# Weights' sums in three steps, queued by hand behind VectorE's products of later query units

## The chip, the cores and the metric

One core of one Trainium2 chip. The metric is the device time of one execution in microseconds; lower is better. Engines: TensorE (PE, with its weight load PEld), VectorE (DVE), ScalarE (ACT), GpSimd (POOL) and SyncE (SP), which issues the transfers.

## The reference

Two layers over a sequence of 1024 rows of width 1024 in float32: first windowed attention with a gate, then a gated linear recurrence (HGRN2) with 8 heads of 128 x 128 state. The second layer is where the change lies:

```
def hgrn2_mixer(h, lower_bound, w_in, gnorm_w, w_out):
    proj = h @ w_in
    q, f, i, z = jnp.split(proj, [FORGET_DIM, 2 * FORGET_DIM, 2 * FORGET_DIM + REC_WIDTH], axis=-1)
    q = jax.nn.silu(q)
    log_f = jnp.logaddexp(jnp.log(lb), jnp.log1p(-lb) + jax.nn.log_sigmoid(f))
    k = -jnp.expm1(log_f)
    ...
    o = chunked_gated_recurrence(q, k, v, log_f)
    o = o * lax.rsqrt(jnp.mean(o * o, axis=-1, keepdims=True) + NORM_EPS) * gnorm_w
    o = o.reshape(B, T, REC_WIDTH) * jax.nn.silu(z)
    return o @ w_out
```

## The kernel before

Matrix products are made of three float32 products of 128 x 128 by 128 x 512 each, from high and low parts (`acth`, `actl` for activations, `whi`, `wlo` for weights). A weight tile of 128 x 512 is loaded by SyncE into one of four `wraw` tiles (`fetch`), and split by ScalarE (`whi`, L203) and VectorE (`wlo`, L204) into one of ten slots as soon as TensorE has used the slot's former content up.

`mixer1` makes the second layer's recurrence. A *query unit* (`qf_unit`) is one product of 24 matmuls: per head four of them, the query and the gate, each for two halves of the sequence, in the order query, gate, query, gate. ScalarE takes a sigmoid of the PSUM bank, and for the query VectorE multiplies both (L946); that frees the bank, of which there are two for this, for the unit after the next. `rec(h)` is the recurrence of a head: two scans U and V on VectorE (L1013, L1014), products into the query and key (L1015, L1016, L1032 to L1036, L1062, tt), small products of TensorE (psd L1044, pss L1054, psq L1070, transposes pst L1087, psk L1093), the state S (L1097, L1099) and the outputs pso (L1106, L1108), which VectorE multiplies by rstd from GpSimd (L1114). `i_unit` makes the values.

The last two products, by the gate's weights z and the output's weights o, are done in the manner of Strassen and Winograd with seven products in place of eight, so sums of the weights' four quarters are needed. `weight_sums(k, ...)` makes them for a quarter tile k, four for z and four for o: it loads three quarters into the three tiles `p1z` (called b11, b12, b22), makes three sums on VectorE (L1127 or L1129, L1130, L1131), stores them to DRAM (`tz`, `td`), loads the remaining quarter into b12, makes a fourth sum (L1137) and stores it (L1138). The same three tiles serve all eight, and later hold first parts of the product z.

The order of the work is set by the list `plan` and a scheduler, which sorts what it is given by a model of its own; each engine's queue is then run in order. `tc.issue_after(ins)` makes the scheduler put instructions behind `ins` on the queue of its engine. `behind` uses it for the place on SyncE's queue: a tile's transfers stand behind the last weight load issued so far.

Of the kernel before, what the change touches and what calls it, by code (L numbers as in the profile page):

```python
# [18 lines left out]
ALU = mybir.AluOpType  # L19
# [71 lines left out]
def emit(tc, I, out):  # L91
    nc = tc.nc
    v = InOrder(tc, nc.vector)
# [7 lines left out]
    with top:  # L101
# [11 lines left out]
        tz, td, sd = [[dp.tile([4 * P, 512], F32, name=f"{n}{i}") for i in range(4)] for n in ("tz", "td", "sd")]  # L113
# [24 lines left out]
        QZ, QO = (100, 108, 104, 112), (120, 128, 116, 124)  # L138
# [15 lines left out]
        W = {"phase": 0, "pos": 0, "bank": 0, "plan": [], "split": 0, "fetch": 0, "left": {}, "place": {}, "dmas": {}, "split_ins": {}, "free": list(zip(whi, wlo))}  # L154
# [103 lines left out]
        def proj_feat(first, half, tag="mm", then={}):  # L258

            ps = mm(tag=tag)  # L260
            for k in range(NK):
                c = (k % 4) * P
                product(ps, k, weight(first, k // 4, c, c + P), act[k, half])
                used(first + k // 4)
                then.get(k, lambda: None)()
            return ps
# [655 lines left out]
        def mixer1(fast, vo, rp, p1z):  # L922
            def i_unit(c, t):
                ps = proj_nat(52 if c == 0 else 76, t)
                nc.scalar.activation(vo[c][:, t, :], ps, AF.Copy)
# [8 lines left out]
            def qf_unit(h, isf, half):  # L934
                ps = proj_feat(60 + 4 * h + 2 * isf + 8 * (h // 4), half)
                cs = slice(half * 512, (half + 1) * 512)
                if (h, isf) not in qfk:
                    if isf and fast:
                        qfk[h, 1] = Fs[h % 2]
                    else:  # L940
                        qfk[h, isf] = rp.tile([P, T], F32, tag="qf"[isf], bufs=2 if isf else nb3, name="qf")
                dst = qfk[h, isf][:, cs]
                if not isf:
                    sg = rp.tile([P, 512], F32, tag="sg", bufs=2, name="sg")
                    nc.scalar.activation(sg, ps, AF.Sigmoid)
                    v.tensor_tensor(dst, ps, sg, op=ALU.mult)  # L946
                else:
                    if (h, 2) not in qfk:
                        qfk[h, 2] = rp.tile([P, T], F32, tag="k", bufs=nb3, name="kk")
                    kk = qfk[h, 2][:, cs]  # L950
                    lb, ol = lbt[:, 1, h:h + 1], lbt[:, 0, h:h + 1]
                    nc.scalar.activation(dst, ps, AF.Sigmoid)  # L952
                    nc.scalar.activation(kk, ps, AF.Sigmoid, scale=-1.0)
                    nc.gpsimd.tensor_scalar(dst, dst, ol, lb, op0=ALU.mult, op1=ALU.add)  # L954
                    nc.gpsimd.tensor_scalar(kk, kk, ol, 1.0, op0=ALU.mult, op1=ALU.mult)
# [159 lines left out]

            QF = [(0, 0), (1, 0), (0, 1), (1, 1)]
            qf = lambda h: [lambda u=u: qf_unit(h, *u) for u in QF]
            iu = lambda c: [lambda t=t: i_unit(c, t) for t in range(8)]

            def weight_sums(k, quarters, dst, neg):  # L1120

                b11, b12, b22 = p1z
                for q, x in zip(quarters, (b11, b12, None, b22)):
                    if x is not None:
                        nc.sync.dma_start(x, I["w"][q + k])
                if neg:
                    v.tensor_tensor(b22, b12, b22, op=ALU.subtract)  # L1127
                else:
                    v.tensor_tensor(b22, b22, b12, op=ALU.subtract)  # L1129
                v.tensor_tensor(b12, b12, b11, op=ALU.subtract)  # L1130
                v.tensor_tensor(b11, b11, b22, op=ALU.subtract if neg else ALU.add)  # L1131
                r = slice(k * P, (k + 1) * P)
                for d, x in ((3, b12), (0, b22), (1, b11)):
                    nc.sync.dma_start(dst[d][r], x)
                b21 = b12
                nc.sync.dma_start(b21, I["w"][quarters[2] + k])
                v.tensor_tensor(b21, b21, b11, op=ALU.subtract)  # L1137
                nc.sync.dma_start(dst[2][r], b21)  # L1138

            rc = lambda h: [lambda: rec(h)]  # L1140

            wz, wo = ([lambda k=k, q=q, d=d, n=n: behind(weight_sums, k, q, d, n) for k in range(4)] for q, d, n in ((QZ, tz, True), (QO, td, False)))

            def behind(f, *a):

                with tc.issue_after(W["dmas"][W["fetch"] - 1].ins):
                    f(*a)

            def ahead(h):
                with tc.high_priority(offset=1200):  # L1150
                    rec(h)
# [4 lines left out]
                    first_part(t, p1z[t])  # L1156

            i1 = iu(1)
            plan = iu(0) + qf(0) + ([zeros] if fast else []) + qf(1) + wz[:1] + rc(0) + qf(2) + wz[1:2] + rc(1) + qf(3) + wz[2:3]
            plan += rc(2) + i1[:4] + wz[3:] + i1[4:] + wo[:1] + rc(3) + qf(4) + wo[1:2] + qf(5) + wo[2:3] + rc(4) + qf(6)  # L1160
            plan += wo[3:] + rc(5) + qf(7) + [lambda: ahead(6), first_parts, lambda: ahead(7)]
            for u in plan:
                u()
            if fast:
# [198 lines left out]
        def network(fast):  # L1363
            keep, oc = layer0()
            with pool("vo", "left") as vp:
                vo = [o0.rearrange("p a (b c) -> p (a b) c", b=2), vp.tile([P, 8, 512], F32, name="vo1")]
                with pool("fin0", "right") as fp:
                    output0(oc, fp, vo[1])
                keep.close()
                with pool("p1z", "right") as zp:  # L1370
                    p1z = [zp.tile([P, 512], F32, name=f"p1z{t}") for t in range(3)]
                    with pool("rec", "left") as rp:
                        final1(vo, rp, p1z, mixer1(fast, vo, rp, p1z))
# [109 lines left out]
```

## Time and profile before

| | |
|---|---|
| three runs | 891.12, 892.0, 892.0 us, median 892.0 |
| the profiled execution's own time | 890.71 us |
| its span, from first to last instruction | 889.0 us |
| TensorE busy | 861.7 us (97%) |
| VectorE busy | 645.7 us (73%) |
| ScalarE, GpSimd busy | 453.9, 313.5 us |
| mean granted clock of TensorE | 0.996 |

The weights' sums run from 466.5 us (the first load) to 669.2 us (the last store). An engine's waits are idle time in front of an instruction, put down to what ended it; a matmul's end is modelled, so TensorE's starts tell more than its ends.

### The profile page before, as it was taken

The numbers are of one execution on the slowest core, as the hardware profiler recorded it, in microseconds if no ns is written. First come the engines' busy times: TensorE is split into PE (matmuls) and PEld (weight loads), VectorE is DVE, ScalarE is ACT, GpSimd is POOL, SyncE is SP. The second block draws the span as 40 slices with busy tenths as digits, with TensorE's granted clock in tenths as the row PEclk, the third lists the DMA queues.
The fourth block names the chain that finished last, engine by engine and source line by source line (L and its number), as shares of the span: only waits on it lengthen the run. The fifth ranks groups of instructions, "written<-read, shape, count | busy, mean of one in ns | idle before, by whom it ended". The sixth has DMA issues, their size and how long they took to land.

```text
span 889.0 us, 14613 instructions
## 1 busy us (share of the span) xinstructions
PE 861.7 (97%) x5166; PEld 715.4 (80%) x5166; DVE 645.7 (73%) x1059; ACT 453.9 (51%) x1143; POOL 313.5 (35%) x475
## 2 busy tenths in 40 slices
PE   6999999999999999999999999999998999999995
PEld 5878888888888878788888788888886878887884
DVE  7898887677898436765279777248768966869985
ACT  5645777767788332753322341243242654668441
POOL 4543644655666303310054442114254421000032
PEclk9999999999999999999999999999999999999999
DMA  9766455313232134536213233063340445423244
GB/s 335 278 187 203 130 172 149 92 52 94 57 93 83 48 94 144 180 119 235 86 48 131 84 120 130 25 190 102 124 166 13 142 144 167 140 74 95 94 142 171
DMA packets 72924, 114.12 MB, mean 128 GB/s; under 512 B 7048, under 2 KB 27144, under 8 KB 72840
## 3 DMA queue, kind: packets, MB, share of 16 engines
q1 hardware_dynamic: 72560, 113.01, 39.2%
q8 instruction: 43, 0.70, 0.3%
q14 instruction: 41, 0.34, 0.1%
q10 hardware_dynamic: 280, 0.07, 0.0%
HBM read 81.76 MB, written 29.46 MB: 125 GB/s over the span
## 4 chain that ended last, share of the span: by engine, by line
PE 69%; DVE 16%; DMA 4%; issue 4%; ACT 3%; POOL 2%; SPq 0%; DVEq 0%; POOLq 0%; ACTq 0%
PE psmm L246 39%; PE psmm L88 17%; PE pss L88 3%; PE pso L88 2%; DMA p1z<-in_w 2%; PE pso L1106 2%; PE pst L88 1%; PE pso L1108 1%; DVE U L1013 1%; PE psk L1093 1%; POOL rstd L285 1%; DVE sc L1048 1%; DVE V L1014 1%; DVE kk L1016 1%; DVE qf L1015 1%
## 5 line engine op out<-in xcount | busy, mean ns | idle before, releaser
L246 PE MATMUL psmm<-whi,acth 128*128 128x512 f32 x448 | 176.9, 396 | 2.6 <-ACT o L1221 1.3
L246 PE MATMUL psmm<-wlo,acth 128*128 128x512 f32 x448 | 175.1, 391 | 0.0
L246 PE MATMUL psmm<-whi,actl 128*128 128x512 f32 x448 | 173.8, 392 | 0.0
L204 DVE TENSOR_TENSOR wlo<-wraw,whi 128x512 fp32r<-128x512 f32 x144 | 99.0, 700 | 64.4 <-ACT whi L203 63.7
L203 ACT ACTIVATE whi<-wraw 128x512 fp32r<-128x512 f32 x136 | 83.7, 628 | 82.5 <-PE psmm L246 63.3
L88 PE MATMUL psmm<-acth,whi 128*128 128x512 f32 x272 | 110.7, 407 | 1.7 <-ACT whi L88 1.7
L88 PE MATMUL psmm<-actl,whi 128*128 128x512 f32 x272 | 107.6, 396 | 0.2 <-DVE actl L88 0.2
L88 PE MATMUL psmm<-acth,wlo 128*128 128x512 f32 x272 | 107.7, 396 | 0.0
L246 PE MATMUL psmm<-acth,whi 128*128 128x512 f32 x256 | 101.9, 398 | 2.8 <-DVE qf L946 2.8
L246 PEld LDWEIGHTS psmm<-whi,acth 128*128 128x128 f32 x448 | 84.2, 188 | 20.6 <-DVE y L851 1.9
L246 PE MATMUL psmm<-acth,wlo 128*128 128x512 f32 x256 | 100.5, 393 | 0.0
L246 PE MATMUL psmm<-actl,whi 128*128 128x512 f32 x256 | 100.4, 392 | 0.0
L246 PEld LDWEIGHTS psmm<-whi,actl 128*128 128x128 f32 x448 | 84.1, 188 | 17.3
L246 PEld LDWEIGHTS psmm<-wlo,acth 128*128 128x128 f32 x448 | 84.2, 188 | 16.5
L736 ACT ACTIVATE sm<-sm,st 128x129 f32<-128x129 f32 x128 | 49.9, 392 | 25.9 <-DVE st L734 25.9
L88 PEld LDWEIGHTS psmm<-acth,wlo 128*128 128x128 f32 x272 | 51.7, 190 | 11.7 <-DVE wlo L88 0.2
L88 PEld LDWEIGHTS psmm<-acth,whi 128*128 128x128 f32 x272 | 52.0, 191 | 10.4 <-ACT whi L88 2.0
L246 PEld LDWEIGHTS psmm<-acth,whi 128*128 128x128 f32 x256 | 48.3, 189 | 14.4 <-DVE qf L946 4.4
L88 PEld LDWEIGHTS psmm<-actl,whi 128*128 128x128 f32 x272 | 51.9, 191 | 8.7 <-DVE actl L88 0.7
L246 PEld LDWEIGHTS psmm<-acth,wlo 128*128 128x128 f32 x256 | 48.3, 189 | 10.1
L246 PEld LDWEIGHTS psmm<-actl,whi 128*128 128x128 f32 x256 | 48.4, 189 | 9.5
L954 POOL TENSOR_SCALAR gate<-gate,lbt 128x512 f32<-128x512 f32 x16 | 20.0, 1251 | 90.2 <-ACT gate L952 90.2
(334 smaller groups left out, 1755.8 us busy)
## 6 DMA issues: line engine op xcount, KB each, us to landing
wraw<-in_w SPq DMA_DIRECT2D x124, 256.0 KB
QS<-qd SPq DMA_DIRECT2D x16, 512.0 KB
p1z<-in_w SPq DMA_DIRECT2D x32, 256.0 KB
xr<-in_x SPq DMA_DIRECT2D x8, 512.0 KB
x1d<-xn SPq DMA_DIRECT2D x8, 512.0 KB
tz<-p1z SPq DMA_DIRECT2D x16, 256.0 KB
td<-p1z SPq DMA_DIRECT2D x16, 256.0 KB
wraw<-sd SPq DMA_DIRECT2D x16, 256.0 KB
```

Source lines behind the costliest of these rows:

```text
L88: return (lambda *a, **k: self.tc.keep_in_program_order(f(*a, **k))) if self.on else f
L203: nc.scalar.activation(hi, raw, AF.Copy)
L204: W["split_ins"][i] = v.tensor_tensor(lo, raw, hi.bitcast(F32), op=ALU.subtract)
L246: W["mm"] = pe.matmul(ps, a, b, start=(k == first and i == 0), stop=(k == last and i == 2), skip_group_check=first is None)
L285: W["rstd"] = keep(g.tensor_tensor(r, m, nhalf[:, :width], op=ALU.pow))
L736: W["exp"] = nc.scalar.activation(sm[:, h, :], sm[:, h, :], AF.Exp, bias=nm[:, h:h + 1], scale=-1.0, accum_out=dn[:, h:h + 1])
L954: nc.gpsimd.tensor_scalar(dst, dst, ol, lb, op0=ALU.mult, op1=ALU.add)
L1013: v.tensor_tensor_scan(U, F[:, :T], F1, 0.0, op0=ALU.mult, op1=ALU.add)
L1014: v.tensor_tensor_scan(V[:, ::-1], F[:, T:0:-1], E1[:, ::-1], 0.0, op0=ALU.mult, op1=ALU.add)
L1015: v.tensor_tensor(Q, Q, U, op=ALU.mult)
L1016: v.tensor_tensor(K, K, V, op=ALU.mult)
L1106: nc.tensor.matmul(po[:, i, :], sc[:, c, :], vt[:, c, hc], start=True, stop=(c == 0))
```

## The change

`weight_sums` returns three steps that stand in the plan by themselves: `loads` (three transfers, behind the last weight load on SyncE's queue), `three` (three sums and their stores, and the load of the fourth quarter) and `fourth` (the last sum and its store). `W["q"]` is the last L946; the sums of `three` and `fourth` are put behind it on VectorE's queue. A function `qfs` sets the steps between a head's query units: the fourth step of the tile before and the loads of this tile behind the first unit, the three sums behind the third. Each tile of z goes with heads 1, 2, 3 and the values' units; each tile of o with heads 4 to 7, in place of behind heads 3 to 6; the last fourth sum stands behind all units of head 7. Lines of the new file: the sums L1127, L1129, L1130, L1131 and L1137 are L1134, L1136, L1137, L1138 and L1145 there. What is computed does not change.

```diff
--- before.py
+++ after.py
@@ -943,7 +943,7 @@
                 if not isf:
                     sg = rp.tile([P, 512], F32, tag="sg", bufs=2, name="sg")
                     nc.scalar.activation(sg, ps, AF.Sigmoid)
-                    v.tensor_tensor(dst, ps, sg, op=ALU.mult)
+                    W["q"] = v.tensor_tensor(dst, ps, sg, op=ALU.mult)
                 else:
                     if (h, 2) not in qfk:
                         qfk[h, 2] = rp.tile([P, T], F32, tag="k", bufs=nb3, name="kk")
@@ -1117,34 +1117,44 @@
             qf = lambda h: [lambda u=u: qf_unit(h, *u) for u in QF]
             iu = lambda c: [lambda t=t: i_unit(c, t) for t in range(8)]
 
+            b11, b12, b22 = p1z
+
             def weight_sums(k, quarters, dst, neg):
 
-                b11, b12, b22 = p1z
-                for q, x in zip(quarters, (b11, b12, None, b22)):
-                    if x is not None:
-                        nc.sync.dma_start(x, I["w"][q + k])
-                if neg:
-                    v.tensor_tensor(b22, b12, b22, op=ALU.subtract)
-                else:
-                    v.tensor_tensor(b22, b22, b12, op=ALU.subtract)
-                v.tensor_tensor(b12, b12, b11, op=ALU.subtract)
-                v.tensor_tensor(b11, b11, b22, op=ALU.subtract if neg else ALU.add)
                 r = slice(k * P, (k + 1) * P)
-                for d, x in ((3, b12), (0, b22), (1, b11)):
-                    nc.sync.dma_start(dst[d][r], x)
-                b21 = b12
-                nc.sync.dma_start(b21, I["w"][quarters[2] + k])
-                v.tensor_tensor(b21, b21, b11, op=ALU.subtract)
-                nc.sync.dma_start(dst[2][r], b21)
+
+                def loads():
+                    with tc.issue_after(W["dmas"][W["fetch"] - 1].ins):
+                        for q, x in ((0, b11), (1, b12), (3, b22)):
+                            nc.sync.dma_start(x, I["w"][quarters[q] + k])
+
+                def three():
+                    with tc.issue_after(W["q"].ins):
+                        if neg:
+                            v.tensor_tensor(b22, b12, b22, op=ALU.subtract)
+                        else:
+                            v.tensor_tensor(b22, b22, b12, op=ALU.subtract)
+                        v.tensor_tensor(b12, b12, b11, op=ALU.subtract)
+                        v.tensor_tensor(b11, b11, b22, op=ALU.subtract if neg else ALU.add)
+                    for d, x in ((3, b12), (0, b22), (1, b11)):
+                        nc.sync.dma_start(dst[d][r], x)
+                    nc.sync.dma_start(b12, I["w"][quarters[2] + k])
+
+                def fourth():
+                    with tc.issue_after(W["q"].ins):
+                        v.tensor_tensor(b12, b12, b11, op=ALU.subtract)
+                    nc.sync.dma_start(dst[2][r], b12)
+
+                return loads, three, fourth
 
             rc = lambda h: [lambda: rec(h)]
 
-            wz, wo = ([lambda k=k, q=q, d=d, n=n: behind(weight_sums, k, q, d, n) for k in range(4)] for q, d, n in ((QZ, tz, True), (QO, td, False)))
-
-            def behind(f, *a):
-
-                with tc.issue_after(W["dmas"][W["fetch"] - 1].ins):
-                    f(*a)
+            wz, wo = ([weight_sums(k, q, d, n) for k in range(4)] for q, d, n in ((QZ, tz, True), (QO, td, False)))
+
+            def qfs(h, now, last=None):
+
+                u = qf(h)
+                return u[:1] + ([last[2]] if last else []) + [now[0]] + u[1:3] + [now[1]] + u[3:]
 
             def ahead(h):
                 with tc.high_priority(offset=1200):
@@ -1156,9 +1166,11 @@
                     first_part(t, p1z[t])
 
             i1 = iu(1)
-            plan = iu(0) + qf(0) + ([zeros] if fast else []) + qf(1) + wz[:1] + rc(0) + qf(2) + wz[1:2] + rc(1) + qf(3) + wz[2:3]
-            plan += rc(2) + i1[:4] + wz[3:] + i1[4:] + wo[:1] + rc(3) + qf(4) + wo[1:2] + qf(5) + wo[2:3] + rc(4) + qf(6)
-            plan += wo[3:] + rc(5) + qf(7) + [lambda: ahead(6), first_parts, lambda: ahead(7)]
+            i1 = iu(1)
+            plan = iu(0) + qf(0) + ([zeros] if fast else []) + qfs(1, wz[0]) + rc(0) + qfs(2, wz[1], wz[0]) + rc(1)
+            plan += qfs(3, wz[2], wz[1]) + rc(2) + i1[:1] + [wz[2][2], wz[3][0]] + i1[1:4] + [wz[3][1]] + i1[4:] + [wz[3][2]] + rc(3)
+            plan += qfs(4, wo[0]) + qfs(5, wo[1], wo[0]) + rc(4) + qfs(6, wo[2], wo[1]) + rc(5) + qfs(7, wo[3], wo[2]) + [wo[3][2]]
+            plan += [lambda: ahead(6), first_parts, lambda: ahead(7)]
             for u in plan:
                 u()
             if fast:
```

VectorE's queue at head 2's scan and head 3's first query product (L946). Before:

```order
L1062 TENSOR_TENSOR qf<-qf,tt 128x16x32
L1127 TENSOR_TENSOR p1z_4211<-p1z_4210,p1z_4211 128x512
L1114 TENSOR_TENSOR o_148<-pso,rstd 128x4x128
L1015 TENSOR_TENSOR qf<-qf,U 128x1024
L1025 COPY tt<-U 128x32 x2
L1016 TENSOR_TENSOR kk<-kk,V 128x1024
L1130 TENSOR_TENSOR p1z_4210<-p1z_4210,p1z_4209 128x512
L946 TENSOR_TENSOR qf<-psmm,sg 128x512
L1026 RECIPROCAL tt<-tt 128x64
L1027 TENSOR_TENSOR tt<-tt 128x32
```

After:

```order
L1062 TENSOR_TENSOR qf<-qf,tt 128x16x32
L1114 TENSOR_TENSOR o_148<-pso,rstd 128x4x128
L1015 TENSOR_TENSOR qf<-qf,U 128x1024
L1025 COPY tt<-U 128x32 x2
L1016 TENSOR_TENSOR kk<-kk,V 128x1024
L946 TENSOR_TENSOR qf<-psmm,sg 128x512
L1145 TENSOR_TENSOR p1z_4210<-p1z_4210,p1z_4209 128x512
L1026 RECIPROCAL tt<-tt 128x64
L1027 TENSOR_TENSOR tt<-tt 128x32
```

L1127 and L1130 have left the rows ahead of L946; the fourth sum, L1145, stands right behind it.

VectorE's queue from head 6's second query product to head 6's scan U (vo is the output of head 4). Before, with the last tile of o:

```order
L946 TENSOR_TENSOR qf<-psmm,sg 128x512
L1097 COPY S<-psk 128x128
L1099 SCALAR_TENSOR_TENSOR S<-S,tt,psk 128x128 x6
L1129 TENSOR_TENSOR p1z_4211<-p1z_4211,p1z_4210 128x512
L1130 TENSOR_TENSOR p1z_4210<-p1z_4210,p1z_4209 128x512
L1131 TENSOR_TENSOR p1z_4209<-p1z_4209,p1z_4211 128x512
L1009 COPY F_4221<-gate_4223 128x64
L1137 TENSOR_TENSOR p1z_4210<-p1z_4210,p1z_4209 128x512
L1114 TENSOR_TENSOR vo_3486<-pso,rstd 128x4x128
L1013 SCALAR_TENSOR_TENSOR U<-gate_4223,F_4221 128x1024
```

After, with the third tile of o:

```order
L946 TENSOR_TENSOR qf<-psmm,sg 128x512
L1136 TENSOR_TENSOR p1z_4211<-p1z_4211,p1z_4210 128x512
L1097 COPY S<-psk 128x128
L1137 TENSOR_TENSOR p1z_4210<-p1z_4210,p1z_4209 128x512
L1099 SCALAR_TENSOR_TENSOR S<-S,tt,psk 128x128
L1138 TENSOR_TENSOR p1z_4209<-p1z_4209,p1z_4211 128x512
L1099 SCALAR_TENSOR_TENSOR S<-S,tt,psk 128x128 x5
L1009 COPY F_4221<-gate_4223 128x64
L1114 TENSOR_TENSOR vo_3486<-pso,rstd 128x4x128
L1013 SCALAR_TENSOR_TENSOR U<-gate_4223,F_4221 128x1024
```

The three sums now stand among the rows of the state S, and no fourth sum stands ahead of L1114 and the scan.

VectorE's queue behind head 7's second query product, with splits of the next weights (actl, wlo) and head 5's state S; after:

```order
L946 TENSOR_TENSOR qf<-psmm,sg 128x512
L1136 TENSOR_TENSOR p1z_4211<-p1z_4211,p1z_4210 128x512
L204 TENSOR_TENSOR actl_1_119<-wraw_112,acth_1_118 128x512
L204 TENSOR_TENSOR actl_1_123<-wraw_113,acth_1_122 128x512
L1137 TENSOR_TENSOR p1z_4210<-p1z_4210,p1z_4209 128x512
L204 TENSOR_TENSOR actl_1_127<-wraw_114,acth_1_126 128x512
L204 TENSOR_TENSOR actl_1_131<-wraw_115,acth_1_130 128x512
L1138 TENSOR_TENSOR p1z_4209<-p1z_4209,p1z_4211 128x512
L1062 TENSOR_TENSOR qf<-qf,tt 128x8x64
L1097 COPY S<-psk 128x128
L204 TENSOR_TENSOR wlo_104<-wraw_112,whi_94 128x512
L204 TENSOR_TENSOR wlo_105<-wraw_113,whi_95 128x512
```

Before, the rows from the first split on were there without the three sums. TensorE's queue behind it, at head 7's psd; before:

```order
L1093 MATMUL psk<-vo_3486,yn 128x128
L1044 MATMUL psd<-U,V 32x32 x32
L1054 MATMUL pss<-qf,kk 32x32
L1093 MATMUL psk<-vo_3486,yn 128x128
L1054 MATMUL pss<-qf,kk 32x32
L1093 MATMUL psk<-vo_3486,yn 128x128
```

After:

```order
L1044 MATMUL psd<-U,V 32x32 x32
L1054 MATMUL pss<-qf,kk 32x32 x3
L1093 MATMUL psk<-vo_3486,yn 128x128 x3
L1054 MATMUL pss<-qf,kk 32x32
L1093 MATMUL psk<-vo_3486,yn 128x128
L1054 MATMUL pss<-qf,kk 32x32 x12
```

Head 6's psk and head 7's pss, which took turns one by one, now stand in larger pieces.

## Rows read from the trace of the kernel before

**Rows 1.** The first part of the page: busy us, share of the span, instructions.

```profile
PE 861.7 (97%) x5166; PEld 715.4 (80%) x5166; DVE 645.7 (73%) x1059; ACT 453.9 (51%) x1143; POOL 313.5 (35%) x475
```

**Rows 2.** Who waited for whom, TensorE, 400 to 720 us: us, times, longest.

```profile
PE psq L1070 <- DVE qf L1062: 3.1, 1, 3.1
PE psmm L246 <- DVE qf L946: 2.8, 4, 1.5
PE pso L1106 <- DVE S L1099: 1.0, 1, 1.0
PE psd L1044 <- DVE tt L1030: 0.2, 1, 0.2
```

**Rows 3.** Timeline of TensorE, 505 to 680 us: start, length, instruction, [idle before <-releaser].

```profile
510.06 0.50 PE L246 MATMUL psmm<-acth,whi 128*128 128x512 f32 x1 [1.50 <-DVE qf L946]
...
621.61 0.50 PE L246 MATMUL psmm<-acth,whi 128*128 128x512 f32 x1 [0.64 <-DVE qf L946]
...
676.77 1.08 PE L1070 MATMUL psq<-qf,kk 128*32 128x64 f32 x32 [3.14 <-DVE qf L1062]
```

**Rows 4.** Busy time by stretches of 2 us; the granted clock is behind POOL.

```profile
676.00:678.00 2.00, 1.23 (x33) 1.09 (x34) 1.97 (x3) 0.09 (x1) 0.00 (x0) 0.58 0.00 0
678.00:680.00 2.00, 2.00 (x6) 1.57 (x7) 2.00 (x5) 0.67 (x2) 1.27 (x1) 0.56 0.00 0
```

**Rows 5.** Who waited for whom, VectorE, 400 to 720 us.

```profile
DVE p1z L1137 <- DMA p1z<-in_w: 14.4, 4, 5.1
...
DVE p1z L1129 <- DMA p1z<-in_w: 5.6, 2, 3.2
...
DVE p1z L1127 <- DMA p1z<-in_w: 4.7, 1, 4.7
```

**Rows 6.** Timeline of VectorE, 650 to 690 us.

```profile
660.34 0.69 DVE L1129 TENSOR_TENSOR p1z<-p1z,p1z 128x512 f32<-128x512 f32 x1 [3.21 <-DMA p1z<-in_w]
...
668.51 0.69 DVE L1137 TENSOR_TENSOR p1z<-p1z,p1z 128x512 f32<-128x512 f32 x1 [5.07 <-DMA p1z<-in_w]
...
669.72 2.28 DVE L1013 TENSOR_TENSOR_SCAN U<-gate,F 128x1024 f32<-128x1024 f32 x1
...
675.93 0.69 DVE L1062 TENSOR_TENSOR qf<-qf,tt 128x512 f32<-128x512 f32 x1
...
679.73 0.67 DVE L946 TENSOR_TENSOR qf<-psmm,sg 128x512 f32<-128x512 f32 x1
```

**Rows 7.** Instructions on the tile p1z: duration ns min/median/max, first and last start us.

```profile
L1131 DVE TENSOR_TENSOR p1z<-p1z,p1z x8: 678/692/1594, 483.1 to 662.2; 128x512 f32<-128x512 f32 x8
```

**Rows 8.** Timeline of VectorE, 490 to 525 us.

```profile
508.30 1.10 DVE L1130 TENSOR_TENSOR p1z<-p1z,p1z 128x512 f32<-128x512 f32 x1
509.32 0.68 DVE L946 TENSOR_TENSOR qf<-psmm,sg 128x512 f32<-128x512 f32 x1
```

**Rows 9.** Timeline of GpSimd, 640 to 722 us.

```profile
664.07 1.03 POOL L285 TENSOR_TENSOR rstd<-ms,nhalf 128x4 f32<-128x4 f32 x1
```

**Rows 10.** Groups by line, 400 to 720 us: the split of weights on ScalarE.

```profile
L203 ACT ACTIVATE whi<-wraw 128x512 fp32r<-128x512 f32 x49 | 30.9, 632 | 61.1 <-PE psmm L246 49.9 <-DMA wraw<-tz 7.3 <-DMA wraw<-in_w 2.9
```

**Rows 11.** The chain that ended last, 400 to 720 us: start, us, what.

```profile
401.54 63.16 PE psmm L246 x278
```

**Rows 12.** Timeline of VectorE, 690 to 715 us.

```profile
700.77 2.29 DVE L1013 TENSOR_TENSOR_SCAN U<-gate,F 128x1024 f32<-128x1024 f32 x1 [0.30 <-POOL gate L1010]
...
710.51 0.68 DVE L1114 TENSOR_TENSOR vo<-pso,rstd 128x512 f32<-128x512 f32 x1
```

**Rows 13.** Timeline of TensorE, 600 to 714 us.

```profile
599.74 1.72 PE L1093 MATMUL psk<-o,yn 128*128 128x128 f32 x14
...
703.01 0.39 PE L1108 MATMUL pso<-S,qf 128*128 128x128 f32 x2
...
712.91 0.49 PE L1093 MATMUL psk<-vo,yn 128*128 128x128 f32 x2
...
713.50 0.49 PE L1093 MATMUL psk<-vo,yn 128*128 128x128 f32 x2
```

## The prediction

> **What bounds the kernel now.** The first part of the page was read first: TensorE is busy for 97% of the span [rows 1], so a change that adds and removes no matmul can win only what TensorE waits, or loses in its sequence. Next came the list of who waited for whom, for TensorE between 400 and 720 us, the stretch in which the weights' sums run. The reader should see that all its waits there are for VectorE: 3.1 us for one product of head 5 (L1062), 2.8 us in four waits for the query product (L946), 1.0 us for the state S (L1099), 0.2 us for tt [rows 2]. That is 7.1 us. The timeline of TensorE places the long ones [rows 3]. Behind the longest, in which TensorE did nothing for 3.1 us, the granted clock stands at 0.58 and 0.56 in two stretches of 2 us, that is mostly at 1.2 GHz, the lower of its two levels, and TensorE is busy for 1.23 and 2.00 us of them [rows 4]; at full clock that work takes about 0.57 of the time, so 3.23 x 0.43 = 1.4 us go there. In all, 8.5 us can be touched at TensorE.
>
> Third, what VectorE waits for in the same stretch. Of its waits, 24.7 us are for the loads of the weights' quarters into p1z, seven waits of up to 5.1 us [rows 5]. They are at the head of an in-order queue, so the recurrence's work behind them stands still: at 655 to 680 us the sum L1129 waits until 660.34 and the fourth sum L1137 until 668.51, and the scan U, the product L1062 and the query product L946 follow [rows 6].
>
> **The change, part by part.** All times are against the profiled execution (span 889.0, its own time 890.71); the three runs' median, 892.0, lies 1.3 us above it and is what I state the forecast in.
>
> No instruction is added or removed: the same 32 sums and 64 transfers. A sum takes 0.69 us at the median [rows 7]; their 22 us stay on VectorE, and what counts is their places. The loads are now issued two query units (24 matmuls each, at 63.16 / 278 = 0.227 us apart [rows 11]: 5.5 us) ahead of the three sums, and these stand behind the second L946 of a head, where VectorE mostly waits for weights from ScalarE anyway; the fourth sum stands behind the first L946 of the next head.
>
> (a) *The four waits for L946, 2.8 us.* At 510.06 TensorE waited 1.50 us [rows 3]; L1130, 1.10 us long [rows 8], and L1127, 0.69 us like other sums, stood ahead of L946 in that pass and now don't: 1.8 us earlier, so the wait goes. The same holds for two small waits. At 621.61 (0.64 us, [rows 3]) the order now puts two half products and L1030 ahead of L946, about as much as it takes away; I count half. Term: 2.8 - 0.3 = **2.5 us**, bounds 1.5 and 2.8.
>
> (b) *S, 1.0 us* [rows 2]. S of head 2 stood behind waits of 4.7 us (L1127) and up to 5.1 us (L1137) [rows 5]. The fourth quarter's tile is loaded only when the store of the former content has landed, so the worst for L1145 is one such wait, but it stands several us of other work behind. S comes some 6 us earlier. Term: **1.0 us**, bounds 0 and 1.0.
>
> (c) *Head 5's product, 3.1 us, the clock, 1.4 us, and tt, 0.2 us.* The waits until 660.34 and 668.51 go. Late next is the first output product of head 4, which the order puts ahead of scan U: it needs the rstd that GpSimd ends at 665.10 [rows 9]. So U starts at about 665.2 instead of 669.72. From U's start to the end of L1062 it was 675.93 + 0.69 - 669.72 = 6.9 us [rows 6], so L1062 ends at 672.1; TensorE asked for it at 676.77 - 3.14 = 673.63 [rows 3]. The wait goes with 1.5 us to spare, and the clock should stay up. Then L946: 10.0 us behind U [rows 6], and 0.6 us more since the reciprocal and L1027 now stand ahead of it: 675.8. TensorE, no longer stopped, needs that bank near 676.2, and a start follows L946's by 0.74 us (510.06 [rows 3] against 509.32 [rows 8]): a new wait of about 0.3 us, and as much for head 6's U and V, with one fourth sum ahead of them. Term: 4.7 - 0.6 = **4.1 us**, bounds 2.5 and 4.7.
>
> (d) *The last tile goes to 685 to 705 us.* This is the price. There the queue has no idle: scan U of head 7 started at 700.77 and the outputs of head 5 at 710.51 [rows 12]. Four sums, 4 x 0.69 = 2.8 us, now lie between L946 and these, beside the splits of the next weights; the new order also puts the first output product behind two splits. The last row of head 5's state now stands behind scan V; U goes 2.8 us back to 703.6 and the two scans, 2.3 us each [rows 12], put that row at 708.0. TensorE's last output of head 5 started at 703.01 [rows 13] and now stands 17 matmuls later, at 706.9: 1.1 us. The output product frees the PSUM bank of head 6's psk; it ended at 711.2 and now ends 2.8 us of sums and 1.4 us of splits later, at 715.4, and TensorE comes to that psk at 712.91 [rows 13] + 1.1 = 714.0: 1.4 us. Together 2.5 us, bounds 0 and 5.
>
> Against this stands a gain in TensorE's sequence. Before, head 6's psk and head 7's pss alternate one by one: from psk to psk 713.50 - 712.91 = 0.59 us, while 14 psk in a row take 1.72 us, 0.25 a pair [rows 13]. An alternation costs 0.34 us; there are about six here and as many between pso and psq, 4.1 us. The new order keeps three. Term: 9 x 0.34 = 3.1 us, bounds 0 (if the pieces wait for their inputs anyway) and 4.1. Net of (d): **+0.6 us**, bounds -5 and +4.1.
>
> *Queues passed.* SyncE's queue now has stores of p1z, which wait for VectorE, ahead of weight loads, and a load of b12 that waits for its own store. I cost this at nothing: the splits wait 49.9 us for TensorE to give up slots, and 10.2 us for loads [rows 10], so weights come early. If that cover is gone, a split is late by what one such load took VectorE at most, 5.1 us [rows 5]. On GpSimd nothing new is queued but the order of rstd and copies at head 7.
>
> Sum: 2.5 + 1.0 + 4.1 + 0.6 = 8.2 us, so 890.71 - 8.2 = 882.5 us in a profiled execution, and 892.0 - 8.2 = **883.8 us** as a median.
>
> **Rivals.**
> *The waits move with the last tile (slower).* In 685 to 705 us the loads of the last tile go beside eight weight loads of the next phase. If its two waits come back there at their old size, 3.2 and 5.1 us [rows 5], TensorE, which has no slack there, pays 8.3 us, the 2.5 us of (d), the clock's 1.4 us, and the alternations stay: 12.2 us against the 7.6 of (a) to (c), 4.6 us slower, 896.6 us. It decides once TensorE waits more than 7.6 + 3.1 = 10.7 us in that stage. For it: the size of the old waits. Against it: the three loads are now issued two units early.
> *The loads are late everywhere (not what it says).* If the queue's own stores hold the loads back, VectorE's 24.7 us stay, only in other places: 892 us, within 0.2%. Against it: VectorE never waited over 5.1 us for a load that it met right behind its issue [rows 5], and some 11 us are given.
> *The sums of the last tile are stretched.* The same sum L1131 took from 0.678 to 1.594 us [rows 7], and long ones ran while GpSimd worked on head data. In 685 to 705 us GpSimd has gates and products of two heads; if each of the four sums takes 0.9 us more there, 3.6 us of (d) are added: 883.8 + 3.6 = 887.4 us. For it: the spread in the row. Against it: the median of that row, 0.692. The same time comes out if (a) and (c) reach little more than their lower bounds. The Trainium skill, SBUF — State Buffer (section "SBUF: two separate sides"), says that a VectorE instruction with two SBUF inputs and a GpSimd instruction that reads SBUF exclude each other for the whole of an instruction; by that rule all four would be stretched, and the sum would be 4.6 us in place of 8.2.
> *The last stage is free.* All of 2.8 + 1.0 + 4.7 us, and 3.1 us of alternations with no new wait: 892.0 - 11.6 = 880.4 us.
>
> **How the numbers follow.** Forecast 883.8 (from 882 to 886): 0.46. Sums stretched, 887.4: 0.25. Last stage free, 880.4: 0.13. Late everywhere, 892: 0.08. Waits move, 896.6: 0.08. The range leaves out the last two and spans the rest with their bounds: from 880.0 to 889.0. A comparison of these kernels tells about 0.2%, 1.8 us, from nothing. Faster by more: 0.46 + 0.25 + 0.13 = 0.84; within: 0.08; slower: 0.08.
>
> **What would show it.** After the change VectorE should wait for p1z loads under 3 us in all; TensorE's waits for L946 and for L1062 at head 5 should be gone or under 0.5 us, and the granted clock be 1.00 between 660 and 690 us. Step (d) is right if TensorE shows waits of 2 to 4 us between 695 and 715 us and the pss and psk pieces stand in blocks. Wrong would be: VectorE still at rest before the sums, weights' splits waiting for loads, or TensorE waits past 690 us of over 8 us.

## The result and the profile after

The changed kernel takes 881.24 us (median of 4 runs, 881.09 to 881.38) against 891.56 us before (4 runs, 890.23 to 892.0): ratio 0.9887, 95% interval 0.987 to 0.9904. That is 10.3 us; the forecast was 883.8 us, a gain of 8.2 us.

The profiled execution has a span of 879.4 us, where it was 889.0. The first part of the page, answering [rows 1]; then who waited for whom between 400 and 720 us (us, times, longest), on TensorE as in [rows 2] and on VectorE for the weights' quarters as in [rows 5]:

```profile
PE 856.7 (97%) x5166; PEld 711.6 (81%) x5166; DVE 646.3 (73%) x1059; ACT 454.4 (52%) x1143; POOL 311.6 (35%) x475
```

```profile
PE psmm L246 <- DVE qf L946: 1.3, 1, 1.3
PE psk L1093 <- DVE vo L1114: 1.0, 1, 1.0
PE pso L1106 <- DVE S L1099: 0.8, 1, 0.8
```

```profile
DVE p1z L1145 <- DMA p1z<-in_w: 1.6, 1, 1.6
```

VectorE does the same work, but 24.7 us of waiting for loads are 1.6 us now, and TensorE's 7.1 us of waits are 3.1 us, at three places that are all new. The wait for L1062 and the four for L946 are gone; behind the one new wait for L946 (1.33 us, ended at 673.58) the granted clock stays up, where [rows 4] had 0.58 and 0.56 (busy time by stretches; the clock stands behind POOL's):

```profile
672.00:674.00 2.00, 0.67 (x4) 0.38 (x3) 2.00 (x5) 1.09 (x2) 1.73 (x3) 1.00 0.00 0
674.00:676.00 2.00, 2.00 (x11) 1.63 (x10) 2.00 (x3) 0.00 (x0) 2.00 (x2) 1.00 0.35 128
```

That the gain is real to the end of the work is seen in VectorE's last instruction, of before and of after. It comes 8.16 us earlier. The spans differ by 1.4 us more, since 6.9 us passed from its start to the end of the span before and 5.4 after; over all kernels below this tail was 5.4 to 6.9 us, 5.9 in another execution of the changed kernel (x13), and what sets it stays open.

```profile
882.11 0.75 DVE L1243 SCALAR_TENSOR_TENSOR sc<-sc,rstd,sc 128x512 f32<-128x512 f32 x1
```

```profile
873.95 0.75 DVE L1255 SCALAR_TENSOR_TENSOR sc<-sc,rstd,sc 128x512 f32<-128x512 f32 x1
```

### The profile page after: what moved, and what is told of

It reads as the page before. It is cut to its first block, busy times and chain, and to the rows that moved or that the text cites. A ratio compares the mean times of both kernels' runs of the same rounds, so it can differ in the third digit from the quotient of the medians.

```text
span 879.4 us, 14599 instructions
## 1 busy us (share of the span) xinstructions
PE 856.7 (97%) x5166; PEld 711.6 (81%) x5166; DVE 646.3 (73%) x1059; ACT 454.4 (52%) x1143; POOL 311.6 (35%) x475
## 4 chain that ended last, share of the span: by engine, by line
PE 82%; DVE 7%; issue 3%; POOL 3%; ACT 2%; DMA 2%; DVEq 0%; SPq 0%; POOLq 0%; ACTq 0%
PE psmm L246 47%; PE psmm L88 21%; PE pss L88 3%; PE pso L88 2%; PE psk L1093 1%; PE pst L88 1%; PE pso L1106 1%; DMA wraw<-in_w 1%; POOL rstd L285 1%; PE pso L1108 1%; DVE V L1014 1%; PE pst L1087 1%; DVE U L1013 1%; PE pst L1231 1%; POOL ms L283 1%
## 5 line engine op out<-in xcount | busy, mean ns | idle before, releaser
L88 PEld LDWEIGHTS psmm<-acth,whi 128*128 128x128 f32 x272 | 51.7, 190 | 10.3 <-ACT whi L88 2.0
```

What stands on the lines that cost most here:

```text
L88: return (lambda *a, **k: self.tc.keep_in_program_order(f(*a, **k))) if self.on else f
```

## The experiments

The change has three parts: loads ahead of time (the lead), sums at chosen places of VectorE's queue, and the fourth sum in a step of its own. Each is undone singly below (x8, x2, x12), x1 has early loads alone, and in x4 only the last tile is new. The change also moves tiles to later places of the plan; x6 moves them back to nearly the old ones. The table has the medians and, from the profiled executions, VectorE's waits for p1z and TensorE's for VectorE from 400 us on, in us.

| kernel | median us (runs) | ratio to before, 95% | p1z waits | TensorE's waits |
|---|---|---|---|---|
| before | 891.56 to 892.28 (51 in all) | 1 | 24.7 | 7.1 |
| changed kernel | 881.24 (4) | 0.987 to 0.9904 | 1.6 | 3.1 |
| x4 only the last tile new | 885.25 (5) | 0.9923 to 0.995 | 17.7 | 7.1 |
| x1 loads early only | 887.31 (5) | 0.9939 to 0.9966 | 22.1 | 6.7 |
| x2 not queued by hand | 891.77 (11) | 0.9988 to 1.0014 | 19.5 | 8.9 |
| x8 no lead | 896.86 (5) | 1.0035 to 1.0063 | 18.6 | 12.0 |
| x12 two steps | 890.28 (12) | 0.996 to 0.999 | 12.1 | 8.0 |
| x7 all sums out | 880.45 (4) | 0.9846 to 0.989 | none | 1.1 |
| x6 one step earlier | 882.68 (4) | 0.9886 to 0.9916 | 10.6 | 1.9 |
| x9 before, in blocks | 889.97 (11) | 0.9971 to 0.9991 | 26.2 | 9.9 |
| x10 x6 in blocks | 881.54 (4) | 0.9864 to 0.9894 | 10.5 | 3.6 |
| x11 query product first | 881.96 (4) | 0.9873 to 0.9903 | 1.5 | 3.4 |
| x13 changed kernel again | 881.65 (4) | 0.9858 to 0.99 | 2.5 | 3.3 |

**x4, the last tile alone.**

```diff
-            plan += wo[3:] + rc(5) + qf(7) + [...]
+            plan += rc(5) + u7[:1] + [n3[0]] + u7[1:3] + [n3[1]] + u7[3:] + [n3[2]] + [...]
```

(`n3` holds the three steps of the change for this tile, `u7` head 7's query units)

> The kernel before, with only the last tile of o made in three steps at head 7; the other seven tiles as before. Theory: terms (c) and (d) of the prediction come out alone, 4.1 + 0.6 = 4.7 us, so 886.8 us, with TensorE's waits of head 5's product gone, the clock at 1.00 behind it, and new waits of 2 to 3 us between 690 and 715 us. Rival (the gain belongs to all tiles alike, an eighth each): about 1.3 us, 890.2 us. Rival (the last tile's price in the last stage eats its gain): 891 us.

It took 6.6 us off; in the trace, last VectorE instruction against last, 4.5 us, and 5.5 us counted from 647 us, since the run was 1.07 us late there by chance; 4.7 us were expected. One tile of eight brings nearly two thirds of the gain (6.6 of 10.3 us by the medians, 5.5 of 8.5 by the trace): the rival of equal shares falls. TensorE's waits from 640 us on are the expected ones:

```profile
PE pso L1106 <- DVE S L1099: 1.0, 1, 1.0
PE psk L1093 <- DVE vo L1114: 0.9, 1, 0.9
PE psd L1044 <- DVE tt L1030: 0.6, 1, 0.6
PE psmm L246 <- DVE qf L946: 0.3, 1, 0.3
```

**x1, the loads alone.**

```diff
-            plan = ... + qf(1) + wz[:1] + rc(0) + qf(2) + wz[1:2] + ...
+            plan = ... + qfl(1, lz[0]) + wz[:1] + rc(0) + qfl(2, lz[1]) + wz[1:2] + ...
```

> The kernel before, with the three loads of a tile's quarters issued two or three query units earlier and nothing else: the sums stay undivided at their old places in the plan, placed by the scheduler. Theory (waits for loads hold VectorE's queue): the 10.3 us of VectorE's waits at L1129 and L1127 go; the 14.4 us at the fourth sum, whose load still follows its own stores, stay. The longest wait of TensorE (3.1 us for L1062) shrinks by about 3 us and the others partly, so 3 to 5 us faster, 887 to 889 us. Rival (what counts is where the sums' own 22 us of work stand in VectorE's queue, the loads don't matter): within 1 us of the kernel before, 891 to 892 us.

The time is as expected, the reason isn't. VectorE still waits 22.1 us, because the scheduler also set the sums earlier, and TensorE 6.7 us. The 3.1 us wait and the clock behind it are gone, but two new waits of 2.0 us have come, with the clock down behind one of them (480 to 484 us):

```profile
PE psmm L246 <- DVE qf L946: 3.7, 3, 2.0
PE pso L1106 <- DVE S L1099: 2.0, 1, 2.0
```

Some turns in the last stage (below) are gone too. The profiled execution is the slowest of the five (889.01 us), and its last VectorE instruction comes only 0.9 us earlier than before the change. So where the 4.5 us of the medians come from stays open, and x1 doesn't show that early loads are worth them.

**x2, without queueing by hand.**

```diff
-                    with tc.issue_after(W["q"].ins):
-                        v.tensor_tensor(b12, b12, b11, op=ALU.subtract)
+                    v.tensor_tensor(b12, b12, b11, op=ALU.subtract)
```

(the same for the three sums)

> The changed kernel without the queueing by hand: the three steps stand in the plan where the change put them, but the scheduler places the sums on VectorE's queue by its own model, often ahead of a query product. Theory (loads issued early count most, the exact place on VectorE's queue counts where a load still follows its own stores): VectorE's waits for loads lie between 1.6 us (changed kernel) and 22.1 us (loads early, sums undivided), and the time between theirs, 884 us (882.5 to 886). Rival (queueing by hand adds nothing once there are three steps): 881.3 us, as the changed kernel. Rival (the place on the queue is all that counts): 887 us or more.

The whole gain is gone, so my theory of a time in the middle fell, and the rival that the place on the queue decides came nearest; that the place isn't all is seen in x8. Left alone, the scheduler sets the sums earlier (the first tile's fourth sum starts at 459.74 us, in the changed kernel at 477.83), and they wait for their loads again, the fourth worst of all (L1143; the first sums are L1133 and L1135):

```profile
DVE p1z L1143 <- DMA p1z<-in_w: 12.5, 5, 5.0
...
DVE p1z L1135 <- DMA p1z<-in_w: 6.4, 2, 3.3
...
DVE p1z L1133 <- DMA p1z<-in_w: 0.6, 1, 0.6
```

**x8, without the lead.**

```diff
-                return u[:1] + ([last[2]] if last else []) + [now[0]] + u[1:3] + [now[1]] + u[3:]
+                return u[:1] + ([last[2]] if last else []) + u[1:3] + [now[0], now[1]] + u[3:]
```

(and the same in the plan for the tile among the values' units)

> The changed kernel with the three loads of a tile issued right ahead of its three sums (behind the third query unit) in place of two units earlier; steps and queueing by hand stay. Theory (VectorE stands still behind a sum that waits for its load, whatever its place): seven or eight waits of up to 5 us for loads come back behind a head's second query product, right ahead of the next head's scans, and TensorE waits for query products and S again: 3 to 6 us slower than the changed kernel, 884 to 887 us. Rival (behind a query product the queue has slack, so the lead isn't needed): within 1 us of the changed kernel, 881 to 882 us.

It is 5 us slower than before the change, 10 us above the range expected: the sign of the whole change hangs on the lead of two units. VectorE's waits are no longer than expected (18.6 us), but they stand ahead of rows of S, splits of weights and copies for the scans, and TensorE's sum to 12.0 us, three of them of 1.93 us and more with the clock down behind:

```profile
DVE p1z L1134 <- DMA p1z<-in_w: 7.9, 3, 4.0
DVE p1z L1136 <- DMA p1z<-in_w: 6.2, 3, 2.6
...
DVE p1z L1145 <- DMA p1z<-in_w: 4.5, 2, 4.2
```

```profile
652.00:654.00 2.00, 0.43 (x2) 0.00 (x1) 1.97 (x5) 1.08 (x2) 1.48 (x1) 1.00 0.00 0
654.00:656.00 2.00, 1.64 (x5) 1.32 (x6) 2.00 (x3) 0.00 (x0) 2.00 (x3) 0.67 0.00 0
656.00:658.00 2.00, 2.00 (x6) 1.63 (x5) 2.00 (x4) 0.00 (x0) 1.92 (x3) 0.50 0.35 131
```

**x12, two steps.** The fourth sum follows the three in the plan.

```diff
-                return u[:1] + ([last[2]] if last else []) + [now[0]] + u[1:3] + [now[1]] + u[3:]
+                return u[:1] + [now[0]] + u[1:3] + [now[1], now[2]] + u[3:]
```

(and the same in the plan for the tile among the values' units)

> The changed kernel in two steps: the fourth sum follows its tile's three sums in the same place of the plan, which puts it ahead of the next head's scan U on VectorE's queue, in place of behind that head's first query product. Theory (a sum that follows its own stores and load holds the queue): VectorE's waits for p1z rise from 1.6 us to 8 to 20 us in four to seven waits, the scans behind them come later, and TensorE waits for query products again; 3 to 6 us slower than the changed kernel, 884 to 887 us. Rival (the lead of the three loads and the place of the three sums carry the gain, the third step is for nothing): within 1 us of the changed kernel, 881 to 882 us.

VectorE's waits are as expected, the time is 3 us worse than the range. At 711 and 713 us TensorE waited 1.48 and 1.58 us, nearly on end, and then ran at half the clock for 7 us:

```profile
710.00:712.00 2.00, 0.22 (x2) 0.14 (x2) 2.00 (x5) 0.00 (x0) 0.32 (x1) 1.00 0.29 70
712.00:714.00 2.00, 1.24 (x9) 0.93 (x9) 0.89 (x3) 0.94 (x4) 0.00 (x0) 0.93 0.78 244
714.00:716.00 2.00, 2.00 (x32) 1.49 (x30) 1.92 (x5) 2.00 (x8) 0.00 (x0) 0.50 0.51 136
716.00:718.00 2.00, 2.00 (x24) 1.60 (x13) 1.94 (x4) 1.88 (x8) 1.53 (x2) 0.50 0.26 95
718.00:720.00 2.00, 2.00 (x6) 1.57 (x5) 2.00 (x5) 1.19 (x3) 1.48 (x2) 0.50 0.61 137
```

In x8 and x12 the expectation left out the same term, the clock; in x8 TensorE's waits alone, 8.9 us more than in the changed kernel, are already over the 3 to 6 us expected. With the clock the trace adds up: against the changed kernel x12 has 4.9 us more of waits and 3.4 us of clock (stretches at 0.93, 0.50 and, from 720 to 725 us, 0.95, their length times what is missing to 1), 8.3 us, and its last VectorE instruction starts 8.34 us later; x8 has 8.9 + 4.8 = 13.7 us, measured 14.2.

**x7, the sums left out.**

```diff
-                        v.tensor_tensor(b12, b12, b11, op=ALU.subtract)
+                        if sums:
+                            v.tensor_tensor(b12, b12, b11, op=ALU.subtract)
```

(the same for the three sums; `sums` is false)

> The changed kernel with all 32 sums left out and every transfer kept, so what is left is what the sums' own work on VectorE still costs. Theory (in their new places the sums cost only the 0.8 us for S and 1.0 us for the output product, and without them the scheduler lets TensorE's small products take turns again, 3 us): 880 to 883 us, no faster than 1 us below the changed kernel. Rival (22 us of sums still delay VectorE's recurrence here and there): 878 us or less.

About 1 us below the changed kernel. TensorE's waits are 2.0 us less, and some turns came back, so the 22 us of VectorE's work may cost 2 us rather than 1; the rest of it is hidden. How much the turns took back here is not shown by a run of its own.

**x6, x9 and x10, the turns on TensorE** (small products of two kinds one by one). x6 moves tiles to the values' units (i1), so that none is in the last stage; x9 and x10 put one piece of TensorE's queue in order, in the kernel before and in x6:

```diff
-                for c in range(8):
+                with tc.issue_after(W["psk"].ins) if h == 7 else nullcontext():
+                    for c in range(8):
...
```

> The changed kernel, with two tiles (the last of z and the first of o) among the eight units of the values, and the other tiles of o one head earlier, so that no sum stands in the last stage. Theory: TensorE's waits for L946 at head 7 (1.3 us), S (0.8 us) and the output product (1.0 us) go, but the scheduler takes turns again between psk and pss and between psq and pso, some 7 turns of 0.34 us: net 0.7 us faster than the changed kernel, 880.5 us. Rival (turns cost nothing): 3.1 us faster, 878.1 us. Rival (eight sums beside the values' units stop TensorE there, where VectorE frees no bank early): over 2 us slower than the changed kernel, 883 us or more.

> The kernel before, with one order on TensorE's queue: head 7's pss stand behind the last psk of head 6. By that, six psk stand in one piece in place of six, and psq is cut into three pieces in place of six; VectorE's queue is almost as before. Theory (taking turns between two kinds of small products costs TensorE 0.34 us each time): about 9 turns fewer, 3 us, so 888.5 us. Rival (the small products come one by one because their inputs do, and a block waits for its last input): within 1 us of the kernel before, with a wait of TensorE for VectorE ahead of the block.

> The kernel with the tiles one step earlier (882.7 us), and head 7's pss behind the last psk of head 6 on TensorE's queue. Theory (a turn costs 0.34 us, but TensorE that comes earlier then waits for S and for the query product, as where the same was done to the kernel before: 3.1 us of turns saved, 2.1 us of new waits): 1 us faster, 881.7 us. Rival (without sums in the last stage VectorE has S and the query product ready): 3 us faster, 879.7 us.

x6 is slower than the changed kernel, not faster, but 9 us below the kernel before: the later places of the tiles are not what gains. Both are alike up to head 6's psd (677.6 and 677.5 us); then x6 has none of the waits of 0.79 and 1.02 us, and still ends 1.28 us later (875.23 against 873.95). What is left for its turns is 1.28 + 1.81 - 0.1 = 3.0 us. Timeline of x6:

```profile
706.02 0.49 PE L1093 MATMUL psk<-vo,yn 128*128 128x128 f32 x2
706.44 0.25 PE L1054 MATMUL pss<-qf,kk 128*32 128x32 f32 x2
706.62 0.49 PE L1093 MATMUL psk<-vo,yn 128*128 128x128 f32 x2
```

From psk to psk 0.60 us; in blocks the same four matmuls take some 0.24 us (14 psk in 1.48 us, 32 pss in 0.39, from start to start). x9 takes such turns out of the kernel before and gains 1.9 us, not 3, by the medians; from head 6's first psk to the end of its trace it gains 1.0 us. The saved time returns in part as waits for VectorE, 2.1 us. The rival expected such waits, but no gain over 1 us:

```profile
723.07 0.49 PE L1071 MATMUL psq<-qf,kk 128*32 128x64 f32 x18 [0.60 <-DVE qf L1063]
724.70 0.71 PE L1107 MATMUL pso<-vo,sc 128*128 128x128 f32 x4 [1.13 <-DVE S L1100]
...
727.28 0.49 PE L1107 MATMUL pso<-vo,sc 128*128 128x128 f32 x2 [0.41 <-DVE S L1100]
```

x10 came out as expected, 1.1 us below x6, with 2.1 us of new waits at the same places, level with the changed kernel. No version with the sums beats that one.

**x11, the new wait for L946.**

```diff
-                v.tensor_tensor(K, K, V, op=ALU.mult)
+                with tc.issue_after(W["q", 7, 0].ins) if h == 6 else nullcontext():
+                    v.tensor_tensor(K, K, V, op=ALU.mult)
```

> The changed kernel with head 6's product of key and V (1.2 us on VectorE) behind head 7's first query product in place of ahead of it. Theory (the 1.33 us for which TensorE waits there come from what stands ahead of L946, and the key's product has slack): the wait goes, and some of it comes back at head 6's psd, which is reached earlier; 0.5 to 1.2 us faster than the changed kernel, 880.0 to 880.8 us. Rival (L946 waits for its sigmoid or its product anyway): the same as the changed kernel, 881.2 us. Rival (head 6's psd is late by as much): 881.2 us too, with a wait at psd of about 1.2 us.

The wait went, and came back whole at psd; the last rival holds. That points to the chain from scan U on as what is late there, not to the place of one product in it.

```profile
678.51 0.68 PE L1046 MATMUL psd<-U,V 128*32 128x32 f32 x54 [1.47 <-DVE V L1037]
```

**x13, the changed kernel again.**

> The changed kernel once more, beside the two others. Theory (most of the spread from run to run of the kernel before, 890 to 893 us, comes from loads that VectorE's queue waits for, and these are gone): 881.2 us with a spread of under 1 us. Rival (the spread is chance and comes back with more runs): 881 to 883 us with a spread of 2 us or more.

The eight runs of it lie within 1.5 us (880.97 to 882.47), the 51 of before within 4.9 us (889.45 to 894.35), x2's within 5.3 and x12's within 6.2. The spread hasn't vanished, so neither theory nor rival came out. The runs are unequal in number, and x6, in which VectorE waits 10.6 us for loads, spreads over only 1.3 us: that such loads make the spread is not shown.

## Why the prediction was right

The mechanism is the predicted one, by the trace; the time itself, 881.24 us, lies below the 882 to 886 us that I gave the forecast, though inside the whole range, and is nearest to a rival that the trace rejects (below). Times of the same instruction before and after show where the gain lies. The execution after was 0.36 us late at 401.9 us, before the stage begins.

- *(a) and (b), 2.5 + 1.0 us.* The product that waited at 621.61 [rows 3] starts at 618.17: 3.44 + 0.36 = 3.8 us. Right, and the wait at 621.61, counted as half gone, is gone; the fourth of the waits of (a), 0.34 us at 646.12, lies in the next stretch.
- *(c), 4.1 us.* To head 5's psk (691.39, then 684.42) another 3.5 us. The long wait and its clock are gone as said. The new wait is 1.33 us in place of 0.3 + 0.3. U stands where I put it, behind L1114 and GpSimd's rstd, and started at 661.26 (665.2 less the 3.4 us gained by then is 661.8); the scan V behind it took 3.08 us, 0.8 more than the 2.27 us of head 7's, and that was not in the sum:

```profile
660.65 0.69 DVE L1114 TENSOR_TENSOR vo<-pso,rstd 128x512 f32<-128x512 f32 x1 [2.79 <-POOL rstd L285]
661.26 2.28 DVE L1013 TENSOR_TENSOR_SCAN U<-gate,F 128x1024 f32<-128x1024 f32 x1
663.46 3.08 DVE L1014 TENSOR_TENSOR_SCAN V<-gate,E 128x1024 f32<-128x1024 f32 x1
...
672.85 0.68 DVE L946 TENSOR_TENSOR qf<-psmm,sg 128x512 f32<-128x512 f32 x1
```

- *(d), +0.6 us.* From there to the end 1.2 us. The waits are 1.02 us at psk and 0.79 us at S, 1.8 in place of 2.5; the turns are worth the 3.0 us that x6 shows, 3.1 in the sum.
- *Queues passed, nothing.* From 400 us on ScalarE waited longer for weights (whi for in_w 7.3 us in place of 2.9), and TensorE never did. Right.

The sum of 8.2 us thus stands against 8.5 us in the trace. Less the 0.36 us that is 8.16 us at VectorE's last instruction. That they meet so closely is in part luck: (c) was 0.6 us too high, (d) 0.6 and (a) with (b) 0.3 us too low, so three misses cancel. The other profiled execution of the changed kernel (x13), 0.90 us late at 402 us, has its last VectorE instruction at 874.79, which makes 8.2 us. The time came out 2.6 us lower by two things outside the sum. 1.4 us are the tail behind the last instruction. The other 1.2 us are the step from the profiled execution to the median: I carried the 1.3 us of before over as fixed, and after it is 0.15 us (881.09 to 881.24). x9 suggests what they are: where its order is still the one of before it waits 1.19 us for L946 at 646.88, the profiled execution before 0.34; but this is argued from one pair of runs.

Two of the signs I had named failed. The wait for L946 was to be gone or under 0.5 us and is 1.33 us, and the waits between 695 and 715 us were to be 2 to 4 us and are 1.8. The others came: 1.6 us of VectorE's waits for p1z, no wait for L1062, the clock at 1.00 from 660 to 690 us, psk and pss in larger pieces.

Of the rivals, "the last stage is free" gave 880.4 us, 0.8 us from the measured time, but it fails: 1.8 us of new waits stand in that stage, and the time came out low by the tail and the step to the median. "The loads are late everywhere" fails with 1.6 us of 24.7 left. "The waits move" needed 10.7 us of waits in the last stage; it has 1.8. x8 shows that the lead is what holds it off: without it the time is this rival's, 896.9 us, though the waits come back all over the stages and not in the last one. "The sums are stretched" fails: the last tile's sums took 0.68, 0.69, 0.68 and 1.01 us, the last one beside a gate on GpSimd, which was at rest during the others. The rule of the Trainium skill (SBUF — State Buffer, "SBUF: two separate sides") isn't spoken against by that; what was wrong is that GpSimd would be busy there. The trace agrees with the rule at head 6, where GpSimd's rstd beside scan V took 2.99 us, for 1.03 in [rows 9], where VectorE stood still:

```profile
664.35 2.99 POOL L285 TENSOR_TENSOR rstd<-ms,nhalf 128x4 f32<-128x4 f32 x1
```

## What to carry to other kernels

In this kernel work that waits for a transfer belonged on an in-order queue where the transfer had landed: give the load its lead, give what follows its own stores a place of its own, and hold both against the scheduler, since undoing any one of the three gave back four fifths of the gain (x12), all of it (x2) or more (x8). Such a wait costs where the engine that bounds the kernel needs the queue's next result (x6 has 10.6 us of it, and TensorE waits 1.9), so count waits at the bounding engine, and add the clock behind the long ones. Removing a wait there also changes the order that a scheduler makes: look at the turns between kinds of small matmuls before and after.

## What the runs showed of the hardware

TensorE's clock after a wait: behind single waits of 1.33 to 1.57 us (changed kernel, before at 510.06, x6, x11, x12) the granted clock stayed at 1.00; behind those of 1.93, 2.01, 2.63, 3.05 and 3.17 us (x8, x2) and 3.14 us (before) it was mostly 0.5, the lower level of 1.2 GHz, for some 3 to 4 us, and 1.4 to 1.7 us were lost each time. The length alone doesn't settle it: in x1 it fell to 0.50 behind a wait of 1.99 us at 480 us and stayed at 1.00 behind one of 1.98 us at 563 us. Nor does it settle the price: in x9 the wait of 3.08 us that ended at 677.51, at the place of the 3.14 us one of before, was followed by 6 us at 0.50, some 3 us lost:

```profile
677.00:679.00 2.00, 1.49 (x33) 1.34 (x34) 1.97 (x3) 0.35 (x1) 0.00 (x0) 0.50 0.00 0
679.00:681.00 2.00, 2.00 (x6) 1.52 (x6) 2.00 (x5) 0.41 (x2) 1.52 (x2) 0.50 0.00 0
681.00:683.00 2.00, 2.00 (x7) 1.52 (x6) 2.00 (x4) 0.17 (x1) 2.00 (x4) 0.50 0.00 0
```

Two waits of 1.48 and 1.58 us nearly on end were followed by 7 us of it (x12). I had met this once, in [rows 4], and taken it as a property of that one place; it is a good part of what made x8 and x12 worse than expected.
